# The last group of a state-space layer: norm factors moved from its activations to its products, and low weight parts at three layer boundaries made on GpSimd

## The chip, the cores and the metric

The kernel runs on one core of a Trainium2 chip. The metric is device time in microseconds (us) of one launch. The engines are TensorE (PE in the profile; its weight loads are PEld), VectorE (DVE), ScalarE (ACT), GpSimd (POOL) and SyncE (SP, which issues the loads of weights).

## The reference, cut to what matters

Two blocks run one after the other on 512 tokens of width 1024: attention, Fourier mixing and experts, then two layers, the first with an S5 mixer and the second with an SSD mixer, each followed by an MLP. The change lies in the second block:

```python
def second_block(x, ...):
    cond = silu(c)
    for i in range(2):
        sh1, sc1, g1, sh2, sc2, g2 = split(cond @ ada_w[i] + ada_b[i], 6)
        h = rmsnorm(x, norm_mix_g[i]) * (1 + sc1) + sh1
        y = s5_mixer(h, ...) if i == 0 else ssd_mixer(h, ...)
        x = x + g1 * y
        h = rmsnorm(x, norm_mlp_g[i]) * (1 + sc2) + sh2
        x = x + g2 * (relu(h @ w1[i]) ** 2) @ w2[i]
    return rmsnorm(x, final_norm_g)

def ssd_mixer(h, ...):
...
    y = y.reshape(bsz, L, M2_D_INNER) * silu(z)
    yg = y.reshape(bsz, L, G, M2_D_INNER // G)                 # G = 4 groups of 512 channels
    yg = yg * rsqrt(mean(yg * yg, axis=-1, keepdims=True) + NORM_EPS)
    y = yg.reshape(bsz, L, M2_D_INNER) * norm_g
    return y @ w_out
```

Each group of 512 channels is normed by itself: one factor for each token and group, `rsqrt(mean + eps)`, between the gated `y` and the product with `w_out`.

## The kernel before, in words

Activations are held with channels on partitions and the 512 tokens along the free axis: `x` is 8 tiles of 128x512. Every f32 product is done in three passes of TensorE. Weights and activations are split into a high part (`wh`, `yh`, `hh`: a copy in the fp32r format) and a low part (`wl`, or the second half of `yh`, or `hl`: value minus high part), and `mm3` multiplies high with high (L157), high weights with the low activation (L158) and low weights with the high activation (L159). A raw block of weights comes in by a load that SyncE issues (four tiles of 128x256, so 128x1024); ACT makes `wh` (L141), and `self.split_eng`, or VectorE where that is None, makes `wl` (L142). Raw blocks have six buffers, and a load may start when the `wl` of the block that held its buffer is made. Before the change GpSimd makes two `wl` in the whole program.

The program in order, in us of the profile: the first block to about 965, the S5 layer to 1190, the first boundary, MLP 0 to 1550, the second boundary, the SSD layer to 1941, the third boundary at 1941 to 2000, MLP 1 and the end.

A **boundary** is where one layer's last products, the sum into `x`, the norm over channels and the next layer's first products meet. `boundary` works in two halves of 256 tokens, th = 0 and 1:

- `last()` gives `products` and `rest`, four of each for an `out_halves` (n = 0 to 3, each of 256 channels). `products[n](th)` fills a PSUM tile `pt`; `rest[n](th, pt)` adds it into `x` with the layer's gate (`residual`, VectorE at L1415, one input in PSUM) and squares the new `x` (ACT, `sq`), and VectorE adds the squares into `acc` (L1284).
- `rstd` sums `acc` over partitions on TensorE (`pss`, L1257), and VectorE works out the reciprocal root (`nv`, L1260; L218 and L219; three times L221, L222, L223): 12 tiny instructions in a row, each needing the one before. `token_bcast` spreads the factors over the partitions on TensorE (`bc`, L1271).
- `norm_half` makes `t` (VectorE, L1305), `hh` (ACT, L1307) and `hl` (VectorE, L1308) for k = 0 to 7. In the first half the `rest` of the second half's products lies between them.
- `fs` are the next layer's first weights, split into a pool of six buffers, which `out_halves` at the third boundary uses too.

The instructions of an engine run in the order in which the scheduler of the tile framework lists them; the source sets data dependences and some priorities, so an instruction can stand far from its place in the source. In `mix` (one SSD group) VectorE makes decay masks (L2023, L2025) for four pairs of heads, m = 0 to 3, and GpSimd multiplies `ec` (L2019) and `xdd` (L1999); TensorE sums into `py`; beside it, as `side`, TensorE does the next group's input products and the group before's output products. At the end of a group come `sumsq`, `rstd_bcast`, `t` (L2045), the high part of `yh` (ACT, L2046) and the low part (VectorE, L2047).

## Time and profile before

| | us |
|---|---|
| median of 3 runs (lowest, highest) | 2353.33 (2344.57, 2357.10) |
| profiled execution, device time | 2356.19 |
| its span on the core | 2354.4 |
| TensorE busy | 2225.7 (95%) |
| VectorE busy | 1362.8 (58%) |
| ACT busy | 819.0 (35%) |
| GpSimd busy | 238.1 (10%) |

All times of single instructions come from that one profiled execution, in us from the start of its span. The granted clock of TensorE is given as a share of full speed (1.00 is 2.4 GHz, 0.50 is 1.2 GHz); its mean over the span is 0.97. Busy time says little by itself: an engine that nothing waits for may be slow for nothing. What matters is the idle time of TensorE and the name of what ended it.

### The profile page before, as it was taken

The page shows a single profiled execution, that of the slowest core. Times are in us where ns is not written, and L with a number is a line of the kernel's source. Part 1 is how long each engine was busy: PE and PEld are TensorE (multiplying, and loading weights), DVE is VectorE, ACT ScalarE, POOL GpSimd, SP SyncE. Part 2 cuts the span into 40 slices and gives each one's busy share as a digit, 9 for nine tenths or more (in the row PEclk, how much of TensorE's full clock was granted, in tenths as well). Part 3 has the DMA queues.
Part 4 walks back from the last instruction along what each step waited for, and adds up shares of the span by engine and source line. Part 5 has one row for each costly group of instructions (what it writes and reads, how often), then busy time and mean ns, then how long its engine had stood idle before and what let it go on. Part 6 is the DMA issues. An engine that isn't in the chain of part 4 may idle for free.

```text
span 2354.4 us, 32104 instructions
## 1 busy us (share of the span) xinstructions
PE 2225.7 (95%) x12448; PEld 1627.6 (69%) x12448; DVE 1362.8 (58%) x2585; ACT 819.0 (35%) x1321; POOL 238.1 (10%) x407
## 2 busy tenths in 40 slices
PE   7989998799999999888999999999999998999997
PEld 4665677354444444587697887888777878888887
DVE  4754555334443444647378885566796778544554
ACT  4322444121122111533242333346754534223232
POOL 0257000011211110100000000000121110000000
PEclk9889998899999999998999999999999999999998
DMA  8566325599999999667837763333333322233230
GB/s 293 145 207 215 110 68 208 202 357 395 396 403 402 397 396 416 202 169 207 263 123 236 233 211 97 109 84 91 108 108 90 109 71 90 81 99 96 92 99 36
DMA packets 254606, 454.02 MB, mean 193 GB/s; under 512 B 22596, under 2 KB 201556, under 8 KB 229876
## 3 DMA queue, kind: packets, MB, share of 16 engines
q1 hardware_dynamic: 245232, 435.25, 53.6%
q0 software_dynamic: 8464, 16.27, 2.1%
q8 instruction: 99, 1.62, 0.3%
q10 hardware_dynamic: 756, 0.43, 0.1%
q14 instruction: 55, 0.45, 0.1%
HBM read 436.15 MB, written 15.74 MB: 192 GB/s over the span
## 4 chain that ended last, share of the span: by engine, by line
PE 67%; DVE 7%; ACT 3%; issue 2%; DMA 2%; SPq 1%; POOL 0%; ACTq 0%; DVEq 0%; POOLq 0%
PE pt L157 13%; PE pt L158 13%; PE pt L159 13%; PE G L1035 5%; PE U L1035 5%; PE Y L1086 5%; PE pcmb L999 2%; PE pg L946 2%; PE pg L947 1%; PE pcmb L1000 1%; DVE wl L142 1%; ACT wh L141 1%; PE pkt L1641 1%; DVE x L1415 1%; PE pk L158 1%
## 5 line engine op out<-in xcount | busy, mean ns | idle before, releaser
L142 DVE TENSOR_TENSOR wl<-w,wh 128x1024 fp32r<-128x1024 f32 (+2 forms) x239 | 287.4, 1208 | 216.8 <-ACT wh L141 212.7
L141 ACT ACTIVATE wh<-w 128x1024 fp32r<-128x1024 f32 (+1 forms) x241 | 248.6, 1040 | 468.4 <-PE pt L158 380.6
L157 PE MATMUL pt<-hh,wh 128*128 128x512 f32 (+2 forms) x976 | 363.3, 377 | 3.2 <-ACT hh L1307 3.0
L158 PE MATMUL pt<-hl,wh 128*128 128x512 f32 (+2 forms) x976 | 362.6, 374 | 0.0
L159 PE MATMUL pt<-hh,wl 128*128 128x512 f32 (+2 forms) x976 | 360.5, 372 | 0.0
L157 PE MATMUL pt<-ab,wh 128*128 128x512 f32 (+1 forms) x576 | 211.8, 372 | 5.2 <-ACT o L1435 2.9
L158 PE MATMUL pt<-ab,wh 128*128 128x512 f32 (+1 forms) x576 | 211.5, 369 | 0.3 <-DVE ab L1384 0.2
L159 PE MATMUL pt<-ab,wl 128*128 128x512 f32 (+1 forms) x576 | 211.2, 368 | 0.0
L157 PEld LDWEIGHTS pt<-hh,wh 128*128 128x128 f32 (+1 forms) x976 | 181.6, 188 | 41.3 <-issue 4.8
L158 PEld LDWEIGHTS pt<-hl,wh 128*128 128x128 f32 (+1 forms) x976 | 182.6, 188 | 34.0 <-issue 3.2
L159 PEld LDWEIGHTS pt<-hh,wl 128*128 128x128 f32 (+1 forms) x976 | 182.8, 188 | 32.7 <-issue 1.7
L1415 DVE SCALAR_TENSOR_TENSOR x<-pt,mod,x 128x512 f32<-128x512 f32 (+1 forms) x184 | 122.3, 678 | 107.7 <-PE pt L159 107.3
L157 PEld LDWEIGHTS pt<-ab,wh 128*128 128x128 f32 x576 | 108.8, 191 | 29.6 <-ACT ab L1383 9.0
L158 PEld LDWEIGHTS pt<-ab,wh 128*128 128x128 f32 x576 | 110.0, 191 | 19.4 <-DVE ab L1384 1.9
L159 PEld LDWEIGHTS pt<-ab,wl 128*128 128x128 f32 x576 | 109.8, 191 | 17.6
L1002 DVE TENSOR_TENSOR x<-x,pcmb 128x512 f32<-128x512 f32 x128 | 83.2, 682 | 64.1 <-PE pcmb L1000 64.1
L1035 PE MATMUL G<-w,xg 128*64 128x512 f32 x512 | 116.9, 598 | 0.0
L1035 PE MATMUL U<-w,xg 128*64 128x512 f32 x512 | 116.7, 598 | 0.0
L2019 POOL TENSOR_TENSOR ec<-ec,BC 128x384 f32<-128x384 f32 x32 | 39.4, 1246 | 690.0 <-DMA bcs<-csd 538.7
L1638 DVE TENSOR_TENSOR dd<-dd,cst 16x64 f32<-16x64 f32 x16 | 3.4, 212 | 138.7 <-DMA dd<-in_s_d 138.7
L946 PE MATMUL pg<-oh,h2h 128*128 128x256 f32 x256 | 65.9, 295 | 15.5 <-DVE oh L933 12.4
L1035 PEld LDWEIGHTS U<-w,xg 128*64 128x64 f32 x512 | 34.1, 136 | 66.9 <-issue 61.5
(581 smaller groups left out, 4222.5 us busy)
## 6 DMA issues: line engine op xcount, KB each, us to landing
w<-in_w_gate SPq DMA_DIRECT2D x64, 1024.0 KB
w<-in_mlp_w SPq DMA_DIRECT2D x128, 512.0 KB
w<-in_w_up SPq DMA_DIRECT2D x63, 1024.0 KB
extra<-in_w_down SPq DMA_DIRECT2D x32, 1024.0 KB
w<-in_w_down SPq DMA_DIRECT2D x31, 1024.0 KB
adaw<-in_ada_w SPq DMA_DIRECT2D x48, 512.0 KB
adaw<-in_ada_w SPq DMA_DIRECT2D x96, 256.0 KB
w<-in_m_w_in SPq DMA_DIRECT2D x40, 512.0 KB
```

The lines of the kernel that those rows point to most:

```text
L141: nc.scalar.activation(h, w, AF.Copy)
L142: (eng or nc.vector).tensor_tensor(l, w, h.bitcast(F32), op=SUB)
L157: nc.tensor.matmul(out, ah, bh, start=start, stop=False, skip_group_check=True)
L158: nc.tensor.matmul(out, ah, bl, start=False, stop=False, skip_group_check=True)
L159: return nc.tensor.matmul(out, al, bh, start=False, stop=stop, skip_group_check=True)
L946: self.pin(nc.tensor.matmul(pt[:, i], self.h2h[:, t, ks], oh2d[:, t], start=(t == 0), stop=False))
L999: pin(nc.tensor.matmul(pt, ls, yh[:, hf], start=True, stop=False))
L1002: nc.vector.tensor_tensor(xs, xs, pt, op=ADD)
L1035: pin(nc.tensor.matmul(pt[64 * i:64 * i + 64], xg[:, kh * 4 + k, so + 64 * i:so + 64 * i + 64], ws[i][:, k], start=(kh == 0 and k == 0), s ...
L1086: pin(nc.tensor.matmul(Y[hf][64 * i:64 * i + 64], hT[:, 2 * kh + k, 64 * i:64 * i + 64], ws[i][:, k, hf * 512:(hf + 1) * 512], start=(kh = ...
L1415: self.nc.vector.scalar_tensor_tensor(xs, src, gate, xs, op0=MUL, op1=ADD)
L2019: nc.gpsimd.tensor_tensor(ec, ec, BC[:, 1, 128:512], op=MUL)
```

## The change

1. In `boundary`, the low parts of the next layer's first weights are made on GpSimd: four `wl` of 128x1024 at the first and at the third boundary, two of 128x1024 and one of 128x256 at the second.
2. In `out_halves`, where it follows the SSD layer (n_norm = 512), the `wl` of n = 1 and n = 3 are made on GpSimd as well; those of n = 0 and n = 2 stay on VectorE.
3. In the last SSD group, `yh` is made without the token factors, one m at a time inside `mix`: the high part by ACT (scaled by the channel's norm weight), the low part by one VectorE instruction. The four `t` and the `rstd_bcast` at the end of `mix` are gone for this group.
4. The factors come in at the results: in `out_halves`, `rstd(512)` is called behind the first half's products of n = 0, the broadcast behind those of n = 1, and ACT copies it to SBUF (`by`). Each `pt` is multiplied by `by` on VectorE into `ptn` (128x512, eight in all), and the residual reads `ptn` (SBUF) in place of `pt` (PSUM). The first half's `rest` of n = 0 is held until that of n = 1.

```diff
--- before.py
+++ after.py
@@ -1344,7 +1344,10 @@
                     if k == (self.at_k[n][i]):
                         with tc.issue_after(iv.ins):
                             rest[i](1, ps[i])
+
+            self.split_eng = self.nc.gpsimd
             fs = [self.halves(w2d, 0, c0, hx, w, nm) for c0, w, nm, _ in blocks]
+            self.split_eng = None
             outs = [[al((w, 512), name="pt") for _ in range(nm)] for _, w, nm, al in blocks]
             for th in range(2):
                 for i, (f, os_) in enumerate(zip(fs, outs)):
@@ -1392,23 +1395,47 @@
                 for m in range(2):
                     self.residual(2 * n + m, pts[m], mod[:, 40 + 2 * n + m:41 + 2 * n + m], False)
 
-    def out_halves(self, w2d, r0, yx, gate):
-
-        fs = [self.halves(w2d, r0, n * 256, yx, K=4) for n in range(4)]
-
-        def products(f):
+    def out_halves(self, w2d, r0, yx, gate, n_norm=0, by=None):
+
+
+        r, held = [], []
+        fs = []
+        for n in range(4):
+
+            self.split_eng = self.nc.gpsimd if n_norm and n % 2 else None
+            fs.append(self.halves(w2d, r0, n * 256, yx, K=4))
+        self.split_eng = None
+
+        def products(n):
             def g(th):
                 pt = self.psum((128, 2, 256), name="pt")
-                f(th, [pt[:, 0], pt[:, 1]], [True, False])
+                fs[n](th, [pt[:, 0], pt[:, 1]], [True, False])
+                if n_norm and th == 0 and n == 0:
+                    r.append(self.rstd(n_norm))
+                if n_norm and th == 0 and n == 1:
+                    self.nc.scalar.activation(by, self.token_bcast(r[0], self.psum_s), AF.Copy)
+                    r.append(by)
                 return pt
             return g
 
+        def add(n, th, pt):
+            if n_norm:
+                t = self.nrm.tile([128, 512], F32, tag="sq", name="ptn").rearrange("p (m n) -> p m n", m=2)
+                self.nc.vector.tensor_tensor(t, pt, r[1][:, None, self.half(th)].to_broadcast([128, 2, 256]), op=MUL)
+                pt = t
+            for m in range(2):
+                self.residual(2 * n + m, pt[:, m], gate[:, 2 * n + m:2 * n + m + 1], c=self.half(th))
+
         def rest(n):
             def g(th, pt):
-                for m in range(2):
-                    self.residual(2 * n + m, pt[:, m], gate[:, 2 * n + m:2 * n + m + 1], c=self.half(th))
+                if n_norm and th == 0 and n == 0:
+                    held.append(pt)
+                    return
+                if held:
+                    add(0, 0, held.pop())
+                add(n, th, pt)
             return g
-        return [products(f) for f in fs], [rest(n) for n in range(4)]
+        return [products(n) for n in range(4)], [rest(n) for n in range(4)]
 
     def residual(self, k, src, gate, last=True, c=slice(0, 512)):
         xs = self.x[:, k, c]
@@ -2004,6 +2031,8 @@
                 else:
                     tt(p8(prev[:, c]), p8(prev[:, c - 1]), cdec[:, c, hs, None].to_broadcast([128, 8, 64]), op=MUL)
                     tt(prev[:, c], prev[:, c], pt, op=ADD)
+            if g == 3:
+                yh = self.B((128, 8, 512), F32R, name="yh")
             for m in range(4):
                 next(side, None)
                 y = self.psum_s(name="py")
@@ -2035,11 +2064,20 @@
                                              stop=True, tile_position=(0, 64 * j), skip_group_check=True)
                 stt(xs[:, m], xs[:, m], dcol[:, 4 * g + m:4 * g + m + 1], y, op0=MUL, op1=ADD)
                 tt(sz[:, m], sz[:, m], xs[:, m], op=MUL)
+                if g == 3:
+
+                    gm = self.col["m2g"][:, 12 + m:13 + m]
+                    nc.scalar.activation(yh[:, m], sz[:, m], AF.Copy, scale=gm)
+                    stt(yh[:, 4 + m], sz[:, m], gm, yh[:, m].bitcast(F32), op0=MUL, op1=SUB)
                 self.sumsq(sz[:, m], m)
+            if g == 3:
+                for _ in side:
+                    pass
+                return [(yh[:, k], yh[:, 4 + k]) for k in range(4)]
             bc = self.rstd_bcast(512)
             for _ in side:
                 pass
-            yh = pool.tile([128, 8, 512], F32R, tag="yh", name="yh", bufs=1) if g < 3 else self.B((128, 8, 512), F32R, name="yh")
+            yh = pool.tile([128, 8, 512], F32R, tag="yh", name="yh", bufs=1)
             for m in range(4):
                 t = pool.tile([128, 512], F32, tag="t2", name="t")
                 stt(t, sz[:, m], self.col["m2g"][:, 4 * g + m:4 * g + m + 1], bc, op0=MUL, op1=MUL)
@@ -2070,8 +2108,10 @@
         for g in range(4):
             nxt = new() if g < 3 else None
             yx = mix(g, *cur, beside(g, cur[1], yx, nxt))
-            cur = nxt
-        return lambda: self.out_halves(a["m2_w_out_2"][0], 3 * 512, yx, mod[:, 16:24])
+            last, cur = cur[1], nxt
+
+        by = last[:, 0]
+        return lambda: self.out_halves(a["m2_w_out_2"][0], 3 * 512, yx, mod[:, 16:24], 512, by)
 
 
     def program(self):
```

In VectorE's order the SSD layer's end and the third boundary read as follows before (here `yh_16092` and `XZ_14840` are the last group's activations, `bc_16053` the spread factors, `wl_16118`, `16124`, `16130`, `16136` the weights of n = 0 to 3):

```order
L223 SCALAR_TENSOR_TENSOR nry_16040<-nrt_16041,nry_16040 128x4
L1415 SCALAR_TENSOR_TENSOR x_7773<-pt_16059,mod1_10262,x_7773 128x512
L2045 SCALAR_TENSOR_TENSOR t_16093<-XZ_14840,cols2_380,bc_16053 128x512
L2045 SCALAR_TENSOR_TENSOR t_16097<-XZ_14840,cols2_380,bc_16053 128x512
L2047 TENSOR_TENSOR yh_16092<-t_16093,yh_16092 128x512
L2045 SCALAR_TENSOR_TENSOR t_16101<-XZ_14840,cols2_380,bc_16053 128x512
L2047 TENSOR_TENSOR yh_16092<-t_16097,yh_16092 128x512
L2045 SCALAR_TENSOR_TENSOR t_16105<-XZ_14840,cols2_380,bc_16053 128x512
L2047 TENSOR_TENSOR yh_16092<-t_16101,yh_16092 128x512
L2047 TENSOR_TENSOR yh_16092<-t_16105,yh_16092 128x512
L142 TENSOR_TENSOR wl_16118<-w_16115,wh_16117 128x1024
L142 TENSOR_TENSOR wl_16124<-w_16121,wh_16123 128x1024
```

After, from the second of the root's instructions behind `nv`; `wl_16084` and `wl_16096` are the weights of n = 0 and n = 2:

```order
L142 TENSOR_TENSOR wl_16084<-w_16081,wh_16083 128x1024
L219 TENSOR_SCALAR nry_16138<-nri_16137 128x4
L221 SCALAR_TENSOR_TENSOR nrt_16139<-nv_16135,nry_16138 128x4
L222 TENSOR_TENSOR nrt_16139<-nrt_16139,nry_16138 128x4
L223 SCALAR_TENSOR_TENSOR nry_16138<-nrt_16139,nry_16138 128x4
L221 SCALAR_TENSOR_TENSOR nrt_16139<-nv_16135,nry_16138 128x4
L142 TENSOR_TENSOR wl_16096<-w_16093,wh_16095 128x1024
L222 TENSOR_TENSOR nrt_16139<-nrt_16139,nry_16138 128x4
L223 SCALAR_TENSOR_TENSOR nry_16138<-nrt_16139,nry_16138 128x4
L221 SCALAR_TENSOR_TENSOR nrt_16139<-nv_16135,nry_16138 128x4
L222 TENSOR_TENSOR nrt_16139<-nrt_16139,nry_16138 128x4
L223 SCALAR_TENSOR_TENSOR nry_16138<-nrt_16139,nry_16138 128x4
```

The `t` and the low parts are gone from here, two `wl` stand inside the chain of the root; the next row is the first `ptn`. Before, the first `wl` stood behind the low parts of `yh`.

GpSimd's program at its end, before:

```order
L2019 TENSOR_TENSOR ec_15930<-ec_15930,BC_14839 128x384
L2019 TENSOR_TENSOR ec_15995<-ec_15995,BC_14839 128x384
L2019 TENSOR_TENSOR ec_16004<-ec_16004,BC_14839 128x384
L2144 UNCONDITIONAL_BRANCH
L2144 ISA
```

After, where `wl_16090` and `wl_16102` are n = 1 and n = 3 of the SSD layer, and `wl_16466` to `wl_16484` the MLP's first four:

```order
L2048 TENSOR_TENSOR ec_16002<-ec_16002,BC_14839 128x384
L2048 TENSOR_TENSOR ec_16011<-ec_16011,BC_14839 128x384
L142 TENSOR_TENSOR wl_16090<-w_16087,wh_16089 128x1024
L142 TENSOR_TENSOR wl_16102<-w_16099,wh_16101 128x1024
L142 TENSOR_TENSOR wl_16466<-w_16463,wh_16465 128x1024
L142 TENSOR_TENSOR wl_16472<-w_16469,wh_16471 128x1024
L142 TENSOR_TENSOR wl_16478<-w_16475,wh_16477 128x1024
L142 TENSOR_TENSOR wl_16484<-w_16481,wh_16483 128x1024
```

Six `wl` follow the last `ec` directly.

TensorE behind the products of n = 1, after (`pt_16151` is n = 1, `pt_16201` n = 2, first half):

```order
L159 MATMUL pt_16151<-yh_15707,wl_16090 128x256
L157 MATMUL pt_16151<-yh_15707,wh_16089 128x256
L158 MATMUL pt_16151<-yh_15707,wh_16089 128x256
L159 MATMUL pt_16151<-yh_15707,wl_16090 128x256
L1271 MATMUL bc_16176<-cst_67,nry_16138 128x128 x4
L157 MATMUL pt_16201<-yh_15707,wh_16095 128x256
L158 MATMUL pt_16201<-yh_15707,wh_16095 128x256
L159 MATMUL pt_16201<-yh_15707,wl_16096 128x256
L157 MATMUL pt_16201<-yh_15707,wh_16095 128x256
```

Before, the broadcast of the factors stood ahead of the first product of n = 0; now it stands between the products of n = 1 and n = 2.

## Rows read from the trace of the kernel before

**Rows 1.** The page: busy time by engine; the chain that ended last.

```profile
PE 2225.7 (95%) x12448; PEld 1627.6 (69%) x12448; DVE 1362.8 (58%) x2585; ACT 819.0 (35%) x1321; POOL 238.1 (10%) x407
...
PE 67%; DVE 7%; ACT 3%; issue 2%; DMA 2%; SPq 1%; POOL 0%; ACTq 0%; DVEq 0%; POOLq 0%
```

**Rows 2.** Windows: length, busy time and count by engine, granted clock, DMA share, GB/s.

```profile
1195.00:1205.00 10.00, 9.81 (x81) 9.40 (x80) 7.94 (x24) 4.02 (x7) 0.00 (x0) 1.00 0.34 97
1205.00:1220.00 15.00, 14.12 (x112) 13.35 (x112) 10.73 (x34) 5.39 (x12) 0.00 (x0) 1.00 0.24 83
1940.00:1950.00 10.00, 3.68 (x16) 2.56 (x15) 9.11 (x19) 5.24 (x7) 0.00 (x0) 0.75 0.01 2
1950.00:1970.00 20.00, 18.45 (x147) 18.11 (x145) 16.55 (x35) 9.36 (x16) 0.00 (x0) 0.95 0.68 211
```

**Rows 3.** Timeline of TensorE: start us, duration, instruction, idle time before and its releaser.

```profile
1925.74 0.54 PE L2030 MATMUL py<-bcs,xd 128*64 128x128 f32 x5 [1.08 <-DVE bcs L2025]
...
1941.57 0.62 PE L1271 MATMUL bc<-cst,nry 128*128 128x128 f32 x4
...
1948.28 0.58 PE L157 MATMUL pt<-yh,wh 128*128 128x256 f32 x1 [6.09 <-ACT wh L141]
...
1990.62 0.74 PE L157 MATMUL pt<-hh,wh 128*128 128x256 f32 x4 [1.11 <-ACT hh L1307]
```

**Rows 4.** Timeline of ACT, third boundary.

```profile
1947.18 5.78 ACT L141 ACTIVATE wh<-w 128x1024 fp32r<-128x1024 f32 x6
...
1957.49 1.06 ACT L141 ACTIVATE wh<-w 128x1024 fp32r<-128x1024 f32 x1 [2.17 <-DMA w<-in_mlp_w]
```

**Rows 5.** Timeline of VectorE, third boundary.

```profile
1942.31 1.41 DVE L2045 SCALAR_TENSOR_TENSOR t<-XZ,cols,bc 128x512 f32<-128x512 f32 x2
...
1948.31 5.77 DVE L142 TENSOR_TENSOR wl<-w,wh 128x1024 fp32r<-128x1024 f32 x5 [0.31 <-ACT wh L141]
...
1953.99 0.87 DVE L1415 SCALAR_TENSOR_TENSOR x<-pt,mod,x 128x256 f32<-128x256 f32 x2
...
1964.55 0.95 DVE L1284 TENSOR_TENSOR acc<-acc,sq 128x256 f32<-128x256 f32 x2
...
1984.88 0.48 DVE L1308 SCALAR_TENSOR_TENSOR hl<-t,mod,hh 128x256 fp32r<-128x256 f32 x1 [0.24 <-ACT hh L1307]
```

**Rows 6.** VectorE beside GpSimd, in two stretches; by line: ns min/median/max.

```profile
1706.70 1.48 POOL L2019 TENSOR_TENSOR ec<-ec,BC 128x384 f32<-128x384 f32 x1 [13.04 <-ACT ec L2018]
...
1707.24 0.96 DVE L223 SCALAR_TENSOR_TENSOR nry<-nrt,nry 128x4 f32<-128x4 f32 x1
...
1719.22 3.51 POOL L1999 TENSOR_TENSOR xdd<-xd,d_dec 128x512 f32<-128x512 f32 x2 [6.73 <-DVE xd L1990]
...
1720.75 0.74 DVE L1415 SCALAR_TENSOR_TENSOR x<-pt,mod,x 128x512 f32<-128x512 f32 x1
...
L223 DVE SCALAR_TENSOR_TENSOR nry<-nrt,nry x36: 152/161/960, 1198.8 to 2347.4; 128x2 f32<-128x2 f32 x24, 128x4 f32<-128x4 f32 x12
...
L2037 DVE TENSOR_TENSOR XZ<-XZ x16: 678/692/1521, 1664.7 to 1935.7; 128x512 f32<-128x512 f32 x16
```

**Rows 7.** Lines of like operations: ns min/median/max, first and last start, forms.

```profile
L142 DVE TENSOR_TENSOR wl<-w,wh x239: 418/1226/1811, 32.8 to 2300.2; 128x1024 fp32r<-128x1024 f32 x117, 128x512 fp32r<-128x512 f32 x2, 128x256 fp32r<-128x256 f32 x1
...
L142 POOL TENSOR_TENSOR wl<-w,wh x2: 2363/2363/2363, 973.7 to 976.0; 128x1024 fp32r<-128x1024 f32 x2
...
L1002 DVE TENSOR_TENSOR x<-x,pcmb x128: 673/680/689, 467.4 to 964.4; 128x512 f32<-128x512 f32 x128
...
L2046 ACT ACTIVATE yh<-t x16: 612/630/635, 1709.9 to 1946.6; 128x512 fp32r<-128x512 f32 x16
```

**Rows 8.** Timeline of VectorE, first and second boundary.

```profile
1198.90 1.23 DVE L142 TENSOR_TENSOR wl<-w,wh 128x1024 fp32r<-128x1024 f32 x1
...
1202.06 0.16 DVE L223 SCALAR_TENSOR_TENSOR nry<-nrt,nry 128x2 f32<-128x2 f32 x1
...
1565.21 1.23 DVE L142 TENSOR_TENSOR wl<-w,wh 128x1024 fp32r<-128x1024 f32 x1
```

## Prediction

> **What bounds the kernel now.** I read the page first. TensorE is busy for 95% of the span and carries 67% of the chain that ended last, VectorE 7%; GpSimd is busy for 10% [rows 1]. So time is to be had only where TensorE stands still, and I went to the three layer boundaries that the change touches. The windows there show TensorE nearly full at the first boundary (9.81 of 10 us, then 14.12 of 15), and one real hole at the third: 3.68 of 10 us between 1940 and 1950, with the granted clock at 0.75 in that window and 0.95 in the next 20 us [rows 2]. TensorE's timeline names the hole: 6.09 us before the first product of SSD's last group, put down to ACT's `wh` [rows 3]. ACT's six `wh` begin only at 1947.18, behind the four `yh` [rows 4], and `yh` waits for the norm factors: VectorE makes `t` from 1942.31 and is through with `yh` just before `wl` at 1948.31 [rows 5]. So the hole is rstd, broadcast, `t` and `yh` in series. Behind the hole the boundary goes by VectorE: first residual 1953.99, last sums of squares 1964.55, last `hl` of the first token half 1984.88 [rows 5]; and TensorE waits for the second half's `hh` (1.11 us at 1990.62) [rows 3]. I therefore sum along VectorE's chain, from the first residual to the last `hl`.
>
> **What is removed: the hole.** With the scale taken out of `yh`, the products can start as soon as the last `yh` and `wh` stand. Four scalings on ACT and four subtractions on VectorE now lie inside the mix, where VectorE is what TensorE waits for (1.08 us for the masks at 1925.74) [rows 3]. A subtraction is 0.7 us (1.41 for two `t` of the same form) [rows 5]. Those of m = 0 and 1 stand ahead of the last masks: 2 x 0.7 = 1.4 us later for the last `py`, and so for group 2's last products, behind which the broadcast now stands at 1941.57 [rows 3]. Taking their end as 1941.3, products start at about 1942.7 instead of 1948.28: 5.6 us earlier (7.0 if the subtractions are hidden, 4.2 if all four, 2.8 us, push).
>
> **What is added: a lock between VectorE and GpSimd.** At 1706.70 GpSimd starts an operation that ends at 1708.18; a step of the reciprocal root on 128x4 numbers, started on VectorE at 1707.24, takes 0.96 us and ends with it, where the median of such steps is 0.161. The longest of the 512-wide products of two SBUF tiles (L2037) is 1.521 against a median of 0.692. Residuals that read PSUM and one SBUF tile are not stretched: 0.74 at 1720.75, in the middle of GpSimd's `xdd` [rows 6]. So a VectorE instruction with two SBUF inputs waits for the end of the GpSimd instruction that runs, and one with a PSUM input doesn't. The Trainium skill, SBUF — State Buffer, section "Who interferes with whom", has the same as a rule: a VectorE instruction with two SBUF inputs and a GpSimd instruction that reads SBUF share a port pair, and whoever issues first blocks the other for its whole length. This case's trace agrees (0.96 for 0.161), and the rule speaks against this change, which gives GpSimd its longest instructions just where VectorE runs its shortest.
>
> GpSimd needs 2.363 us for a `wl`, VectorE 1.226 (medians) and ACT about 1 us for the `wh` before it [rows 4, 7]. So at the third boundary GpSimd's first four `wl` run back to back: with `wh` of n = 1 there at about 1942.4, they end at 1944.8, 1947.2, 1949.6 and 1952.0, as far as VectorE lets them. On GpSimd they stand behind the last `ec` of the mix and nothing waits behind them; SyncE's loads keep their order, but a raw weight buffer comes free only with its `wl`, so a `wl` that GpSimd ends late also starts a load late. VectorE meanwhile has, between `nri` and the last `nry`, 11 instructions with two SBUF inputs: `wl` of n = 0 and n = 2 and nine tiny ones.
>
> **The norm factors, with and without the lock.** Without it: pss at about 1943.5, the 12 tiny steps (0.161 each, 0.2 with the gap) and two `wl` of 1.2 make 4.8 us, factors at 1948.3; the broadcast stands on TensorE behind the products of n = 1 (48 products at 18.45 us for 147 [rows 2] = 6.0 us, from 1942.7 to 1948.7), so it is not held; with 0.5 us for it, and 0.6 for ACT's copy (as the scalings, L2046 [rows 7]), the first `ptn` starts at about 1950.0 and the first residual at 1950.7, 3.3 us before 1953.99. With it: one VectorE instruction slips in between two of GpSimd's. Behind the first comes `wl` of n = 0 (1.2 us, which GpSimd waits out in turn), then one tiny step behind each of the second and third (0.3 together); GpSimd ends the fourth at about 1953.5, the rest of the steps with `wl` of n = 2 take 2.2 more: factors at 1955.7. Were GpSimd's next always ahead of VectorE's, all 11 would wait until 1952.0 and then need 4.2: 1956.2, so it hardly matters who wins. TensorE is then through with n = 0 and 1 at about 1951.5 (n = 0 waits for its `wl`), stands in front of the broadcast, with n = 2 and n = 3 queued behind it, for some 4 us: a new wait in the place of the old. First `ptn` at 1957.0, first residual at 1957.7: **3.7 us later than before**. I take the locked case, since the rows show the lock each time that such an instruction meets a GpSimd one.
>
> **The first token half's residuals.** Before, 1953.99 to 1965.5 [rows 5]. Now VectorE has 4 `ptn` of 0.68 (a 512-wide product with PSUM: L1002 [rows 7]) = 2.7, 8 residuals 3.4, 7 sums 2.9 and two `wl` 2.4, together 11.4 us: from 1957.0 to 1968.4, **+2.9** (without the lock from 1950.0 to 1961.4, -4.1; these durations are means of rows 5 and 7). Reading `ptn` from SBUF costs the residuals nothing by itself, but makes them blockable.
>
> **First norm and second token half.** Four more `ptn`, +2.7; two `wl` (one inside the chain of the root, one behind the first `t`) go to GpSimd, -2.4. Those two on GpSimd fall into that same chain, since their `wh` wait for buffers that th1's products free: each can hold VectorE for 0 to 2.36 us. I take 1.5 for both (0 to 4.7). So **+1.8**. Sum of the third boundary: 2.9 + 1.8 = **+4.7 us**; without the lock -4.1 + 0.3 = -3.8; with both `wl` fully in the way +7.9.
>
> **First boundary.** Two of the four `wl` stood inside the chain of the root, the first at 1198.90, and the chain ended at 1202.2 [rows 8]. ACT ends their `wh` at about 1198.1 and 1200.3. GpSimd's would run from 1198.1 to 1200.4 and on to 1202.8; of the nine steps with two SBUF inputs one or two come before the first, one slips in between, and seven come behind the second, 7 x 0.2 = 1.4: end at 1204.2, 2.0 us later. TensorE is at 9.81 of 10 before 1205 and loses 0.88 in the 15 us after [rows 2], so about half is covered: **+1.0** (+2.2 with no cover; without the lock the chain ends 2.4 us sooner, but TensorE is full, -0.7).
>
> **Second boundary.** One `wl` (1565.21, 1.23 us) stood between the last two steps [rows 8]. GpSimd takes it in 2.36 from the same moment, so the last steps come 1.15 later; TensorE still has other products queued: **+0.3** (-1.2 to +1.2).
>
> **Sum.** 4.7 + 1.0 + 0.3 = +6.0 on the profiled execution's 2356.2, so 2362.2. The median of the three runs shown is 2353.3, 2.9 below the profiled one; on it the change gives 2359.3.
>
> **The rivals.**
> - *The lock does not bite* (GpSimd's `wl` come later or VectorE wins the short gaps). For it: VectorE loses nothing to it with a PSUM operand, and GpSimd has nothing else to do. Against: every meeting of the two in the trace. Then -3.8 - 0.7 - 1.2 = -5.7: 2347.6. Chance 0.22.
> - *The hole only moves.* TensorE needs its 192 products, 24 us at that rate, either way; if the wait before the broadcast is as long as the start is early, and VectorE's later chain is covered by th1's products and the first ones of the MLP, nothing is left: 2353, within 2. For it: TensorE at 18.45 of 20 us behind the hole [rows 2]. Against: `hh` already is waited for. Chance 0.16.
> - *Slower: the chain of the norm factors runs into GpSimd's last two `wl`.* If weights come early enough for the fifth and sixth `wl` to follow the fourth, the nine steps end at about 1959.8, 4 us later than I have it; with the full 2.0 + 1.2 at the other two boundaries that is 4.7 + 4 + 2.2 + 1.2 = +12.1, 2365.4. It decides from the moment that the fifth `wh` ends before 1953. Against it: one `wh` of these waited for its DMA until 1957.49 [rows 4]. Chance 0.14.
> - The forecast: 0.48.
>
> **How the numbers follow.** This kernel's runs lie 12 us apart (2344.6 to 2357.1), and 0.5%, 11.8 us, is about what a measurement can tell from no change. Range: below, the first rival less some of that spread, 2345; above, the third rival with 2 us more, 2368. Slower by over 0.5% (above 2365.1): half of the third rival and a sixth of the forecast, 0.15. Faster (below 2341.6): a quarter of the first, 0.06. The rest, 0.79, is no change that can be told.
>
> **What would show it.** In the profile after: TensorE's wait before the first product of the last group falls from 6.09 to about 1; a new wait of 3 to 5 us before `bc`, released by VectorE's `nry`; steps of 128x4 that take up to 2.4 us while GpSimd runs `wl`; a first `ptn` near 1957 counted from a mix that ends as before. At the first boundary steps of 128x2 that take 1 us and more. I am wrong if the steps keep 0.16 beside GpSimd's `wl`, or if the first residual comes before 1953.

## The result, and the profile after

The changed kernel takes 2369.93 us (median of 5 runs, 2360.79 to 2370.6) against 2350.46 (5 runs, 2344.57 to 2357.1): ratio 1.0070, 95% interval 1.0054 to 1.0086, so 12.7 to 20.2 us slower. The forecast was +6.0 us and "no change that can be told" as the likeliest class, with 2368 as the upper end of the range. The median lies 1.9 us above that end. The sign was right and the size 2.7 times too small (16.5 for 6.0). The profiled execution took 2367.35 us, 11.2 more than that of before.

Both traces hold 12,448 matmuls, so the start of the k-th of one can be laid against that of the k-th of the other. The shift between them (after less before) is nearly a step function, and its steps say where the time went:

| stretch | shift at its start, us | at its end, us | step, us | forecast |
|---|---|---|---|---|
| start to the first boundary | 0 | -4.0 | -4.0 | 0 |
| first boundary | -3.96 | +1.52 | **+5.5** | +1.0 |
| MLP 0 | +1.5 | +1.5 | 0 | 0 |
| second boundary | +1.47 | +5.11 | **+3.6** | +0.3 |
| SSD up to the last group | +5.1 | +5.0 | 0 | 0 |
| third boundary (from the middle of group 3) | +5.03 | +13.09 | **+8.1** | +4.7 |
| MLP 1, end | +13.1 | +11.6 | -1.5 | 0 |

The steps outside the boundaries, -4.0 before any changed instruction and -1.5 at the end, differ from run to run (the runs below have -5.1 to +2.3 and 0 to -1.4 there). The three boundaries, 17.2 us, are the change. Of the first step, 0.6 arises behind the boundary, at TensorE's wait for `ab` at 1277 in MLP 0 (0.66 us before, 1.29 here), which differs from run to run; up to the product that the kernel before starts at 1250 the step is +4.9.

First boundary, VectorE's timeline (start us, duration, instruction, idle time before and its releaser): the steps of the root, beside GpSimd's last two `wl` there.

```profile
1194.26 2.31 DVE L219 TENSOR_SCALAR nry<-nri 128x2 int32<-128x2 int32 x1
...
1196.61 2.25 DVE L221 SCALAR_TENSOR_TENSOR nrt<-nv,nry 128x2 f32<-128x2 f32 x1
...
1200.26 0.16 DVE L223 SCALAR_TENSOR_TENSOR nry<-nrt,nry 128x2 f32<-128x2 f32 x1
```

```profile
1194.16 4.68 POOL L142 TENSOR_TENSOR wl<-w,wh 128x1024 fp32r<-128x1024 f32 x2 [9.80 <-ACT wh L141]
```

The second and third step of the root take 2.31 and 2.25 us in place of 0.17 and 0.16, one for each GpSimd `wl`; the eight that follow are undisturbed. Before, two `wl` of VectorE's own stood here (the first of them is in [rows 8]). TensorE in the same place:

```profile
1193.22 0.61 PE L1257 MATMUL pss<-ones,acc 128*128 128x1 f32 x4
...
1195.80 0.28 PE L159 MATMUL pt<-gh,wl 128*128 128x256 f32 x1
...
1200.48 0.69 PE L1271 MATMUL bc<-cst,nry 128*128 128x128 f32 x2 [4.40 <-DVE nry L223]
```

It ends its last product at 1196.1 and stands 4.40 us before the broadcast. Before, there was no wait at this broadcast, and it stood farther behind the sums of squares:

```profile
1197.18 0.61 PE L1257 MATMUL pss<-ones,acc 128*128 128x1 f32 x4
...
1202.28 0.43 PE L1271 MATMUL bc<-cst,nry 128*128 128x128 f32 x2
```

Second boundary, VectorE, GpSimd and TensorE:

```profile
1566.78 2.21 DVE L223 SCALAR_TENSOR_TENSOR nry<-nrt,nry 128x2 f32<-128x2 f32 x1
```

```profile
1566.63 2.34 POOL L142 TENSOR_TENSOR wl<-w,wh 128x1024 fp32r<-128x1024 f32 x1 [30.19 <-ACT wh L141]
```

```profile
1569.04 0.67 PE L1271 MATMUL bc<-cst,nry 128*128 128x128 f32 x2 [2.20 <-DVE nry L223]
```

Here only the last step of the root waits (2.21 us), and TensorE 2.20 us with it.

Third boundary, VectorE from the last group's factors on, and GpSimd:

```profile
1947.70 1.83 DVE L218 TENSOR_SCALAR nri<-nv 128x4 int32<-128x4 int32 x1
...
1950.58 2.33 DVE L219 TENSOR_SCALAR nry<-nri 128x4 int32<-128x4 int32 x1
...
1952.95 2.29 DVE L221 SCALAR_TENSOR_TENSOR nrt<-nv,nry 128x4 f32<-128x4 f32 x1
...
1955.27 2.32 DVE L222 TENSOR_TENSOR nrt<-nrt,nry 128x4 f32<-128x4 f32 x1
...
1959.82 0.16 DVE L223 SCALAR_TENSOR_TENSOR nry<-nrt,nry 128x4 f32<-128x4 f32 x1
...
1961.42 0.69 DVE L1424 TENSOR_TENSOR ptn<-pt,XZ 128x512 f32<-128x512 f32 x1 [1.44 <-ACT XZ L1416]
...
1962.15 0.88 DVE L1442 SCALAR_TENSOR_TENSOR x<-ptn,mod,x 128x256 f32<-128x256 f32 x2
...
1971.21 2.99 DVE L1442 SCALAR_TENSOR_TENSOR x<-ptn,mod,x 128x256 f32<-128x256 f32 x2
...
1976.46 1.67 DVE L218 TENSOR_SCALAR nri<-nv 128x2 int32<-128x2 int32 x1
...
1998.10 0.48 DVE L1308 SCALAR_TENSOR_TENSOR hl<-t,mod,hh 128x256 fp32r<-128x256 f32 x1
```

```profile
1947.14 10.43 POOL L142 TENSOR_TENSOR wl<-w,wh 128x1024 fp32r<-128x1024 f32 x4 [12.54 <-ACT wh L141]
...
1971.57 2.36 POOL L142 TENSOR_TENSOR wl<-w,wh 128x1024 fp32r<-128x1024 f32 x1 [13.99 <-ACT wh L141]
...
1975.74 2.36 POOL L142 TENSOR_TENSOR wl<-w,wh 128x1024 fp32r<-128x1024 f32 x1 [1.81 <-ACT wh L141]
```

Four steps wait for the four back-to-back `wl` (1.83, 2.33, 2.29, 2.32), the factors stand at 1960.0, the first `ptn` starts at 1961.42. The fifth `wl` holds the last two residuals, which now read SBUF (2.99 us for the two, 0.88 elsewhere), and the sixth the next root (1.67 us). TensorE's timeline, to be laid beside [rows 3]:

```profile
1950.71 0.39 PE L159 MATMUL pt<-yh,wl 128*128 128x256 f32 x1 [2.66 <-DVE wl L142]
...
1960.13 0.62 PE L1271 MATMUL bc<-cst,nry 128*128 128x128 f32 x4 [2.39 <-DVE nry L223]
...
1975.23 1.00 PE L1257 MATMUL pss<-ones,acc 128*128 128x1 f32 x4 [2.85 <-DVE acc L1284]
```

The hole of 6.09 us is gone; in its place TensorE waits 2.66 us for `wl` of n = 0, 2.39 for the broadcast and 2.85 for the sums of squares.

Windows (length, busy time and count by engine, granted clock, DMA share, GB/s), of the first, second and third boundary:

```profile
1195.00:1200.00 5.00, 1.08 (x10) 0.87 (x8) 4.76 (x8) 1.06 (x1) 3.84 (x2) 1.00 0.35 107
...
1200.00:1205.00 5.00, 4.52 (x25) 4.53 (x26) 3.57 (x11) 1.82 (x4) 0.00 (x0) 0.66 0.94 311
...
1570.00:1575.00 5.00, 5.00 (x34) 5.00 (x34) 4.12 (x11) 2.57 (x6) 0.00 (x0) 0.75 0.45 112
...
1975.00:1990.00 15.00, 13.37 (x72) 12.27 (x73) 11.23 (x30) 4.26 (x9) 2.36 (x1) 0.74 0.24 70
```

After the long waits the granted clock is for some us at its lower level (0.50, 1.2 GHz): its mean is 0.66 from 1200 to 1205, 0.75 from 1570 to 1575 and 0.74 from 1975 to 1990, and 1.00 in the same three windows of the kernel before. TensorE then takes 0.21 us for a product of 0.12. That adds 1.4 us to the wait of 4.4 at the first boundary (the shift is +5.8 at 1205, and 0.9 of it is made good by 1220) and 1.4 to the wait of 2.2 at the second.

### The profile page after: what moved, and what is told of

Same layout as the page of the kernel before. It is cut to its first block, busy times and chain, and to the rows that moved or that the text cites. A ratio compares the mean times of both kernels' runs of the same rounds, so it can differ in the third digit from the quotient of the medians.

```text
span 2365.6 us, 32120 instructions
## 1 busy us (share of the span) xinstructions
PE 2228.0 (94%) x12448; PEld 1631.2 (69%) x12448; DVE 1373.7 (58%) x2576; ACT 819.2 (35%) x1322; POOL 271.6 (11%) x420
## 4 chain that ended last, share of the span: by engine, by line
PE 68%; DVE 6%; ACT 3%; issue 2%; DMA 2%; POOL 0%; SPq 0%; ACTq 0%; DVEq 0%; POOLq 0%
PE pt L157 14%; PE pt L158 13%; PE pt L159 13%; PE G L1035 5%; PE U L1035 5%; PE Y L1086 5%; PE pcmb L999 2%; PE pg L946 2%; PE pg L947 1%; PE pcmb L1000 1%; DMA adaw<-in_ada_w 1%; DVE wl L142 1%; ACT wh L141 1%; PE pkt L1668 1%; DVE x L1442 1%
## 5 line engine op out<-in xcount | busy, mean ns | idle before, releaser
L142 DVE TENSOR_TENSOR wl<-w,wh 128x1024 fp32r<-128x1024 f32 (+1 forms) x226 | 273.9, 1215 | 214.6 <-ACT wh L141 210.5
L1442 DVE SCALAR_TENSOR_TENSOR x<-pt,mod,x 128x512 f32<-128x512 f32 (+1 forms) x168 | 115.2, 697 | 106.8 <-PE pt L159 106.5
L142 POOL TENSOR_TENSOR wl<-w,wh 128x1024 fp32r<-128x1024 f32 (+1 forms) x15 | 37.3, 2501 | 512.3 <-ACT wh L141 424.5
```

Source lines behind the costliest of these rows:

```text
L142: (eng or nc.vector).tensor_tensor(l, w, h.bitcast(F32), op=SUB)
L1442: self.nc.vector.scalar_tensor_tensor(xs, src, gate, xs, op0=MUL, op1=ADD)
```

## The experiments

Each kernel was timed as the changed one was; the steps at the three boundaries are read from its profiled execution in the same way. Code that is the same in two runs gave steps that differ by up to 1.6 at the first boundary (the old code: -0.9 to +0.7), by 1.2 at the second and by 2 at the third, so only larger differences are read from this table.

| run | first | second | third | ratio to before (95%) |
|---|---|---|---|---|
| changed kernel | +5.5 | +3.6 | +8.1 | 1.0070 (1.0054 to 1.0086) |
| e1: boundaries' `wl` back on VectorE | +0.2 | -0.1 | +3.2 | 1.0023 (1.0008 to 1.0038) |
| e2: only boundaries' `wl` on GpSimd | +4.1 | +2.4 | +2.0 | 1.0045 (1.0031 to 1.0059) |
| e3: factors moved, nothing on GpSimd | +0.7 | +0.9 | +3.9 | 1.0007 (0.9993 to 1.0022) |
| e4: broadcast later in TensorE's list | +1.3 | +2.1 | +10.0 | 1.0051 (1.0032 to 1.0069) |
| e5: zero fill in place of subtraction | -1.8 | +0.2 | +1.5 | 1.0006 (0.9990 to 1.0022) |
| e6: e3, factors on one half alone | -0.2 | +0.6 | -0.6 | 1.0004 (0.9984 to 1.0024) |
| e8: e3, root first in the lists | -0.9 | +0.8 | +3.7 | 1.0009 (0.9994 to 1.0024) |
| e9: before, `wl` behind the root | -0.7 | +0.3 | +0.8 | 1.0003 (0.9992 to 1.0014) |

At the first two boundaries most of this scatter arises behind the root that matters: at the wait for `ab` at 1277 (1.33 us in e3, none in e8), and behind 1580 in stretches at the lower clock, which the kernel before has too (0.67 on the mean of 1585 to 1590). Up to the products that the kernel before starts at 1250 and at 1580, the same code agrees within 0.1 us:

| step up to | changed | e1 | e2 | e3 | e4 | e5 | e6 | e8 | e9 |
|---|---|---|---|---|---|---|---|---|---|
| 1250 (first) | +4.9 | -0.1 | +4.9 | 0.0 | +2.2 | -0.8 | -0.1 | 0.0 | -0.8 |
| 1580 (second) | +3.6 | 0.0 | +3.5 | 0.0 | +0.9 | +0.1 | 0.0 | 0.0 | 0.0 |

**e1, the boundaries' weights back on VectorE.**

```diff
 boundary (the changed kernel)
-            self.split_eng = self.nc.gpsimd
             fs = [self.halves(w2d, 0, c0, hx, w, nm) for c0, w, nm, _ in blocks]
-            self.split_eng = None
```

> The changed kernel with the low parts of the boundaries' weights back on VectorE; the norm factors on the results and GpSimd's wl of n = 1 and n = 3 stay. Theory (the lock stretches the chain of the norm factors, and TensorE stands in front of a broadcast that its queue holds early): first boundary +0 against before (after: +5.5), second +0 (after: +3.6), third +1, since only two GpSimd instructions (n = 1, n = 3) stand in the chain instead of four, and the two late ones are gone: factors about 4.6 us sooner than in the changed kernel. In all 1 us slower than before, 16 faster than the changed kernel. Rival (moving the factor behind the products is itself the loss: eight more VectorE instructions of 0.68 and a late first residual): the third boundary keeps +6 to +8, the other two 0.

The first two boundaries are as before; the kernel is 11 us faster than the changed one and still 1.9 to 8.9 slower than before. The third boundary keeps +3.2, between the two numbers expected. VectorE's chain there:

```profile
1943.98 1.84 DVE L218 TENSOR_SCALAR nri<-nv 128x4 int32<-128x4 int32 x1
...
1946.87 2.33 DVE L219 TENSOR_SCALAR nry<-nri 128x4 int32<-128x4 int32 x1
...
1951.82 0.16 DVE L223 SCALAR_TENSOR_TENSOR nry<-nrt,nry 128x4 f32<-128x4 f32 x1
```

Two steps wait (1.84 and 2.33 us) for n = 1 and n = 3 in place of four, and the root ends 8.0 us after its `nri` starts, where the changed kernel took 12.3.

**e2, only the boundaries' weights on GpSimd.**

```diff
 boundary (the kernel before)
+            self.split_eng = self.nc.gpsimd
             fs = [self.halves(w2d, 0, c0, hx, w, nm) for c0, w, nm, _ in blocks]
+            self.split_eng = None
```

> The kernel before with only the low parts of the boundaries' weights on GpSimd; the last group's factors stay ahead of the products. Theory (lock and queue): first boundary +5.5, second +3.6, third +2 to +5 (four GpSimd wl beside VectorE's wl and inside the chain of the norm), in all +11 to +14 us against before. Rival (the moved factors are the loss): third boundary 0 or a gain of 1 to 3 us, since VectorE has four wl less.

In all +7.3 to +13.9 us by the median, as the lock would have it, though each boundary in the first table is at or under the low end of what was expected; up to 1250 and 1580 the first two steps are the changed kernel's. TensorE at the first boundary waits to the hundredth as in the changed kernel:

```profile
1206.77 0.69 PE L1271 MATMUL bc<-cst,nry 128*128 128x128 f32 x2 [4.40 <-DVE nry L223]
```

**e4, the broadcast later in TensorE's list.** The chain stays late, but TensorE has products ahead of the broadcast.

```diff
 boundary (the changed kernel; late = 0 at the first boundary, 1 at the second, None at the third)
-            bc = rstd(0)
-            ps = [f(1) for f in products]
...
+            r0 = self.rstd(D, range(2))
...
+            for i, f in enumerate(products):
+                ps.append(f(1))
+                if i == late:
+                    with tc.issue_after(self.last_mm.ins):
+                        bc = self.token_bcast(r0, self.psum_s)[:, 0:256]
```

> The changed kernel, with the first half's broadcast at the first boundary put in TensorE's queue behind all products of the second half, and at the second boundary behind two of four; nothing else is moved. Theory (the lock makes the chain late, but the price is the queue: TensorE stands before the broadcast while it has other products): first boundary +1 to +2 in place of +5.5, second +2 to +2.5 in place of +3.6, the third as in the changed kernel: 4 to 6 us faster than the changed kernel. Rival (the late chain alone costs this, since TensorE runs out of products anyway): first boundary keeps +4.5 or more.

VectorE's chain is stretched as in the changed kernel, and TensorE no longer waits for it:

```profile
1193.15 2.33 DVE L219 TENSOR_SCALAR nry<-nri 128x2 int32<-128x2 int32 x1
```

```profile
1199.84 0.38 PE L1271 MATMUL bc<-cst,nry 128*128 128x128 f32 x2
...
1201.34 0.50 PE L157 MATMUL pt<-hh,wh 128*128 128x256 f32 x2 [1.11 <-ACT hh L1307]
```

The root's step takes 2.33 us and the broadcast waits for nothing; what is left is 1.11 us for `hh` and, at 1206.01, 1.05 us for `sg` (0.21 before). The step of the first boundary falls from +5.5 to +1.3, or from +4.9 to +2.2 up to 1250; that of the second from +3.6 to +0.9 up to 1580. The lock makes the factors 2 us later than before; the other half of the wait of 4.4 us is made by TensorE's list. The scheduler had moved the broadcast: before, 36 products stood between the sums and the broadcast, covering the two `wl` in the chain; with these gone from VectorE it put the broadcast behind 18 (at the second boundary 18 in place of 27), which covers the 2.4 us of an undisturbed root and no more. The third boundary, where nothing was edited, came out at +10.0 against +8.1, and the ratio is 1.0051 against 1.0070, with intervals that overlap.

**e5, a zero fill in place of the subtraction.**

```diff
 split (the changed kernel; fill_low is set around the boundaries' weights)
-        (eng or nc.vector).tensor_tensor(l, w, h.bitcast(F32), op=SUB)
+        if eng is not None and self.fill_low:
+            eng.memset(l.bitcast(F32), 0.0)
+        else:
+            (eng or nc.vector).tensor_tensor(l, w, h.bitcast(F32), op=SUB)
```

> The changed kernel, in which GpSimd fills the low parts of the boundaries' weights with zeros in place of the subtraction (the low parts of these weights are left out of the result): the same number of GpSimd instructions behind the same waits, with nothing read from SBUF. The lists of the engines stay as in the changed kernel. Theory (the lock between two instructions that read SBUF): the steps of the root at the first two boundaries take 0.16 to 0.17 us, TensorE's wait in front of the broadcast at the first falls from 4.4 us to below 0.5, first boundary 0 to -1 against before, second 0; the third keeps the lock of n = 1 and n = 3 and loses that of the other four: +3 to +4. In all about 14 us faster than the changed kernel. Rival (the moved order, with the broadcast 18 rows behind the sums in place of 36, is what costs): first boundary stays at +4 to +5.5.

This is the test of the lock: the lists of TensorE, VectorE and ACT are the changed kernel's row for row. A fill does not wait for `wh`, so the first two run at 1101 (the `wl` at 1178); the others at the first two boundaries stand beside the root, as the `wl` did. The kernel gives back the whole loss: -1.8 at the first boundary where the changed one had +5.5 (-0.8 for +4.9 up to 1250), and +1.5 at the third, less than expected. VectorE beside GpSimd (the first two rows at the first boundary, the third at the third), GpSimd (a row at the first boundary, one at the second, two at the third), and TensorE at the first boundary:

```profile
1196.60 0.16 DVE L228 SCALAR_TENSOR_TENSOR nry<-nrt,nry 128x2 f32<-128x2 f32 x1
...
1196.79 0.16 DVE L226 SCALAR_TENSOR_TENSOR nrt<-nv,nry 128x2 f32<-128x2 f32 x1
...
1941.04 4.11 DVE L224 TENSOR_SCALAR nry<-nri 128x4 int32<-128x4 int32 x1
```

```profile
1196.58 0.95 POOL L145 MEMSET wl<- 128x1024 f32 x1 [1.30 <-PE pt L164]
...
1559.42 0.95 POOL L145 MEMSET wl<- 128x1024 f32 x1 [335.80 <-DVE nrt L227]
...
1937.60 5.75 POOL L147 TENSOR_TENSOR wl<-w,wh 128x1024 fp32r<-128x1024 f32 x2 [12.58 <-ACT wh L143]
...
1943.29 1.83 POOL L145 MEMSET wl<- 128x1024 f32 x2
```

```profile
1197.40 0.43 PE L1276 MATMUL bc<-cst,nry 128*128 128x128 f32 x2 [0.17 <-DVE nry L228]
```

Four steps of the root start inside the fill at the first boundary (1196.58 to 1197.53) and five inside the one at the second; each takes 0.16 us, and TensorE waits 0.17 for the broadcast that it holds in the same place of its list. So it is neither the moved list alone nor GpSimd being busy: it is that both read SBUF. The rival fell. A fill is also shorter (0.95 us for 2.36), but that doesn't explain steps that are not stretched at all.

**e3, the factors alone.**

```diff
 out_halves (with e1's edit)
-            self.split_eng = self.nc.gpsimd if n_norm and n % 2 else None
+            self.split_eng = None
```

> The changed kernel with every wl on VectorE: only the norm factors are moved. Theory (lock): no step of the chain takes more than 0.2 us beside a wl, factors 7 us sooner than in the changed kernel, first residual 3 us ahead of before, third boundary -3 us, the others 0. Rival (the moved factors are the loss): third boundary +2 to +5 from the eight added products and the broadcast in TensorE's queue.

Here my theory fell: without any lock I expected -3 at the third boundary, and in this execution it is +3.9, as the rival said. (The median is +1.6 us over the kernel before, -1.6 to +5.2.) With the `wl` back on VectorE the broadcast also stands behind 63 products, 48 in the changed kernel. VectorE's and ACT's timelines there (on this run's clock, 0.6 us ahead of before):

```profile
1942.18 4.63 DVE L142 TENSOR_TENSOR wl<-w,wh 128x1024 fp32r<-128x1024 f32 x4
...
1955.46 0.87 DVE L1440 SCALAR_TENSOR_TENSOR x<-ptn,mod,x 128x256 f32<-128x256 f32 x2
...
1986.32 0.48 DVE L1308 SCALAR_TENSOR_TENSOR hl<-t,mod,hh 128x256 fp32r<-128x256 f32 x1
```

```profile
1951.50 1.06 ACT L141 ACTIVATE wh<-w 128x1024 fp32r<-128x1024 f32 x1 [6.26 <-DMA w<-in_mlp_w]
...
1952.46 0.58 ACT L1414 ACTIVATE XZ<-bc 128x512 f32<-128x512 f32 x1
```

Four `wl` stand inside the root, two more behind its next steps, and ACT's copy of the broadcast stands behind a `wh` that waited 6.26 us for its load. The first residual comes at 1955.46, 2.0 us later than before after the 0.6 are added, though the products began about 6 us sooner. TensorE is early for nothing:

```profile
1971.38 0.35 PE L157 MATMUL pt<-hh,wh 128*128 128x256 f32 x1 [2.21 <-DVE ptn L1422]
...
1973.14 0.58 PE L157 MATMUL pt<-hh,wh 128*128 128x256 f32 x1 [1.17 <-ACT hh L1307]
```

```profile
1975.00:1980.00 5.00, 4.74 (x20) 4.20 (x20) 4.21 (x11) 2.08 (x6) 0.00 (x0) 0.50 0.00 0
```

It waits 2.21 us for a `ptn`, 1.17 for `hh`, and then works at 0.50 of the clock.

**e8, the root first.** If the place of the factors in the lists is what costs, this mends it.

```diff
 out_halves (the changed kernel; also all wl on VectorE, and the first rest is no longer held)
+        with ExitStack() as c:
+            if n_norm:
+                r.append(self.rstd(n_norm))
+                c.enter_context(self.tc.issue_after(self.last_rs.ins))
+            fs = [self.halves(w2d, r0, n * 256, yx, K=4) for n in range(4)]
...
                 if n_norm and th == 0 and n == 0:
...
+                    with self.tc.issue_after(ip.ins):
+                        bc = self.token_bcast(r[0], self.psum_s)
+                    self.by = self.nc.scalar.activation(by, bc, AF.Copy)
 boundary
...
+            with ExitStack() as c:
+                if self.by is not None:
+                    c.enter_context(tc.issue_after(self.by.ins))
+                fs = [self.halves(w2d, 0, c0, hx, w, nm) for c0, w, nm, _ in blocks]
```

> Only the factors are moved (all wl on VectorE), but the steps of the root stand ahead of all wl on VectorE, the broadcast behind the products of n = 0 on TensorE, and ACT's copy of it ahead of the MLP's wh. Factors then stand at about 2.4 us behind nv in place of 8.6, and the first residual some 4 to 6 us sooner than in the run with the factors alone. Theory A (VectorE's whole work behind the hole sets the end, and the added products take what the hole gave): third boundary +0 to +2 in place of +3.9. Theory B (the place of the factors in the queues is what costs): third boundary -2 to -4 against before, and the kernel is 2 to 4 us faster than before.

```profile
1942.55 0.16 DVE L225 SCALAR_TENSOR_TENSOR nry<-nrt,nry 128x4 f32<-128x4 f32 x1
...
1950.00 0.88 DVE L1439 SCALAR_TENSOR_TENSOR x<-ptn,mod,x 128x256 f32<-128x256 f32 x2
...
1984.75 0.48 DVE L1310 SCALAR_TENSOR_TENSOR hl<-t,mod,hh 128x256 fp32r<-128x256 f32 x1
```

Factors 2.3 us behind `nv`, first residual at 1950.00 (1952.1 on before's clock, 4.0 sooner than e3). And the last `hl` of the first half ends at 1987.3 on before's clock, e3's at 1987.4: nothing is left of the 4.0 us, because VectorE makes in the meantime the `wl` that it had put off: it is idle for 0.1 us of the 13.3 between that residual and the half's last sum of squares. Step +3.7, so theory B fell and A stands, though over its own +0 to +2: what ends last is VectorE's work.

**e6, the factors on one half alone.** The results of the second half's tokens lack their factors here.

```diff
 out_halves, add (with e3's edit)
-            if n_norm:
+            if n_norm and th == 0:
```

> Only the factors are moved (all wl on VectorE), and the second half of the tokens leaves out its product with the factors (the residual reads PSUM; those tokens' sums miss the factor). Theory A (VectorE's chain behind the first residual sets the third boundary, and the added products are what costs): four products less between the first t and the last hl, 4 x 0.68 = 2.7 us, and with them most of TensorE's waits at half clock: third boundary +3.9 falls to about +0.5. Theory B (the late first residual, 2 us behind that of before, is what costs): it stays at +3 or more.

```profile
1952.64 0.87 DVE L1440 SCALAR_TENSOR_TENSOR x<-ptn,mod,x 128x256 f32<-128x256 f32 x2
...
1980.25 0.48 DVE L1308 SCALAR_TENSOR_TENSOR hl<-t,mod,hh 128x256 fp32r<-128x256 f32 x1 [0.24 <-ACT hh L1307]
```

First residual 1952.64 and last `hl` of the first half 1980.25: 27.6 us between them, where e3 has 1986.32 less 1955.46 = 30.9. Four instructions of 0.68 less on VectorE take 4.5 us off the step (+3.9 to -0.6): their own 2.7, and for the rest there is TensorE's time at the lower clock behind 1965, 6.8 us where e3 has 13.7; how the rest divides is not shown. Theory B's +3 did not come.

**e9, the kernel before with its `wl` behind the root.** The version to which the rest pointed.

```diff
 boundary (the kernel before; root is the last step of the first half's root)
-            fs = [self.halves(w2d, 0, c0, hx, w, nm) for c0, w, nm, _ in blocks]
+            fs = [self.halves(w2d, 0, c0, hx, w, nm) for c0, w, nm, _ in blocks[:-1]]
+            with tc.issue_after(root.ins):
+                fs += [self.halves(w2d, 0, c0, hx, w, nm) for c0, w, nm, _ in blocks[-1:]]
```

> The kernel before, all wl on VectorE, where the low parts of the last block of a boundary's first weights are listed behind the last step of the first half's root (they stood inside the chain: two at the first boundary, one at the second). Theory (what stands between the steps, a wl of VectorE's own or a lock, is what delays the broadcast): the chain is 2.4 us shorter at the first boundary and 1.2 at the second; TensorE, which is nearly full at both, keeps 0.5 to 2 us of the first and 0 to 1 of the second: 1 to 3 us faster than before in all, which the median can hardly tell and the offset between the two traces can. Rival (VectorE's work is the same, and the wl are only late elsewhere): 0.

The steps are -0.7, +0.3 and +0.8, the ratio 1.0003: in time nothing. The trace keeps 0.8 us of the shorter chain up to 1250, at the low end of what was expected, and nothing up to 1580; TensorE was nearly full there [rows 2]. The broadcast stands behind 18 products at both, as in the changed kernel: it moves when the `wl` leave the chain, whichever engine makes them. No version was found that beats the kernel before.

## Why the prediction came out as it did

- **The lock**: right, shown by e5. Also its arithmetic: factors forecast at 1955.7 on before's clock, found at 1960.0 - 5.0 = 1955.0; first residual 1957.7 against 1957.1; root of the first boundary +2.0 against 2.2 (1200.4 + 4.0 - 1202.2), of the second +1.15 against 1.0.
- **First and second boundary**: the step that failed is TensorE's cover ("so about half is covered", "TensorE still has other products queued"). I took TensorE's list as it was before. The change had also moved the broadcast from behind 36 products to behind 18, and from 27 to 18. So the wait of 4.4 us is the root's 2.2 and 18 products of 0.12 that no longer stand ahead, the wait of 2.2 the root's 1.0 and 9 products; and the clock, for which the sum has no term, took 1.4 more each time. +1.0 and +0.3 were +5.5 and +3.6. With the products ahead e4 has +2.2 and +0.9 up to 1250 and 1580, so even then the cover was less than forecast. The lists were there to be compared; I compared them at the third boundary alone.
- **Third boundary**: the start was right, though TensorE's wait before the broadcast was 2.39 us and not 3 to 5. Mis-sized is what follows on VectorE (after less before, on before's clock). At the half's last sum the chain is 4.6 late and not 2.9: the fifth `wl` fell there and cost 2.1 (2.99 for 0.88). From there to the last `hl` it loses 3.6 and not 1.8: the sixth `wl` cost 1.5, and VectorE's idle time before `pss`, `bc` and `hh` grew by 1.3, which is no term of the sum. TensorE's clock, at 0.74 for 15 us, is none either; its share is not shown.
- **"Without the lock -3.8"**: wrong, though nothing of the forecast rests on it but the first rival. Without the lock the traces have +3.9 (e3), and with the factors at their earliest +3.7 (e8). I had put the eight `ptn` against the eight instructions removed and let the early first residual carry through to the end; VectorE had no free time in which to use it. So by the traces about half of the third step is the factors, and the rest GpSimd's `wl` of the MLP (e1 to the changed kernel: +4.9). Whether `wl` of n = 1 and n = 3 on GpSimd cost something is open: e3 to e1 is -0.7 at the third boundary, but e1's median is 3.0 us over e3's.
- **Rivals**: "the lock does not bite" is out (e5). "The hole only moves" is out by its number, 2353. "The chain runs into the last two `wl`" named the right two instructions, but they met the last residuals and the next root, not the chain of the last group; that its +12.1 (with 2.2 for the first boundary, where "the full 2.0" is written) lies nearest to 16.5 is luck.

What stays open: the scatter of the third boundary's step (+8.1 and +10.0 in the same code), and why e3's median (+1.6 us, -1.6 to +5.2) is lower than the sum of its steps in one execution (+5.5). By the medians alone the moved factors without the lock (e3, e8) cannot be told from no change.

## What to carry to other kernels

Moving work to an idle engine is not free when it reads SBUF beside short steps on VectorE: each step can cost the whole length of the other engine's instruction, so look for chains of tiny instructions before choosing where long ones go. When an edit shortens a chain in the scheduler's eyes, look where the instruction that waits for the chain now stands in its engine's list. And a hole on one engine is worth only what the engine that ends last can use of it.

## What was not expected of the hardware

- A VectorE step with one SBUF input waits too: `nri` and `nry` (TENSOR_SCALAR on 128x2 or 128x4) took 1.83 and 2.33 us beside a `wl`.
- A zero fill on GpSimd held a TENSOR_SCALAR but no step with two inputs: in e5 `nry` at 1941.04 took 4.11 us, from the end of VectorE's `wl` of n = 0 through GpSimd's of n = 3 to the end of the two fills (1943.29 + 1.83 = 1945.12), while steps of the other forms took 0.16 inside a fill. This is one case. The Trainium skill, SBUF — State Buffer, section "Who interferes with whom", says the same by kind: `tensor_scalar` can enter a mode that takes both of VectorE's port pairs, if its operands meet the conditions, and an instruction with two SBUF inputs contends only with a GpSimd instruction that reads SBUF. This trace agrees with both (4.11 us, and 0.16).
- The waits of 4.40 and 2.20 us before the broadcasts were each followed by some 3 us at the lower clock level (products of 0.21 us in place of 0.12): after 1200.48 until 1203.7, and after 1569.04 until 1572.5.
